# Two modulation vectors of a diffusion layer: matmul sets that take one weight tile each

## The chip, the cores and the metric

The kernel runs on one core of a Trainium2 chip. The time is device microseconds (us) of one launch. A core has TensorE (PE in the profile, its weight loads apart as PEld), VectorE (DVE), ScalarE (ACT), GpSimd (POOL) and a queue from which SyncE (SP) issues the transfers (DMA). TensorE writes its results into accumulator tiles of 128 partitions by 512 numbers.

## What is computed

One layer of a diffusion backbone over 256 latent tokens and 256 context tokens, of width 2048. A vector c of 2048 numbers is turned into six modulation vectors, and one for the context into two:

```python
mod = (jax.nn.silu(c) @ w_ada[i] + b_ada[i])[:, None, :]
mod_c = jax.nn.silu(c_ctx) @ w_ada[i] + b_ada[i]
sh1, sc1, g1, sh2, sc2, g2 = jnp.split(mod, N_MOD, axis=-1)
hc = rmsnorm(h_ctx, norm1_w[i]) * (1.0 + csc1) + csh1
s_f, s_b = ssd_branch(hc, zero_state, zero_state, None, lp, False)
hl = rmsnorm(x, norm1_w[i]) * (1.0 + sc1) + sh1
out_l, _, _ = token_mixer(hl, s_f, s_b, grid, lp)
x = x + g1 * out_l
hl2 = rmsnorm(x, norm2_w[i]) * (1.0 + sc2) + sh2
x = x + g2 * sqrelu_mlp(hl2, w_mlp1[i], w_mlp2[i])
return rmsnorm(x, final_norm_w)
```

The mixer has a long convolution and a state scan side by side. The MLP has 8192 hidden units. All is fp32 in size; a w_ada vector is a product of one row of 2048 with a matrix of 2048 by 2048 numbers (16 MB).

## The kernel before

Everything lies with channels on the 128 partitions and tokens along the tile. The large products (w_in, w_out, the MLP) stream 512 KB tiles of weights through the ring `raw` (5 tiles). Each is split into two reduced-precision parts (`hl`), with which TensorE does three matmuls of 128x128 weights by 256 tokens for each 128x128 block, into tiles `pg`. In the profile these are the rows `pg<-b,hl`; the text calls them the stream.

The modulation vectors come in three ways. The first two (and the context's) are made at the start by `ada_first` from `raw` and `ra` tiles. Vectors 0 and 1 (g1 and sh2) are made by `ada_vector` (line 422), and 2 and 3 by `vector_on_v` (line 443) on VectorE, whose multiply-adds are on line 459.

`ada_vector(v)` goes over 16 blocks kt of 128 inputs. For each it takes two tiles of the ring `ra` (5 tiles of 128x1024, which `vector_on_v` also uses), loads the 2048 output channels of the block into them (line 441), and calls `four` (line 413). That issues four fp32 matmuls, whose weights are 32 columns of the activated c (`csF`, through `cs32`) and whose moving operand is 512 channels of w_ada. The four write the four quarters of 32 partitions of one accumulator `pa` (ring of one tile), quarter j getting the channels 512 j to 512 j + 511, so that each uses its own 32 columns of the array. Only the first of the 32 rows of a quarter is used. In the text such a group of four is a set. After kt = 15 `columns` copies `pa` to a tile `ev` on ScalarE (line 287), and four small matmuls with the constant `sel2` turn rows into columns, in another tile `pa`. `finish` (line 405) adds the bias and writes `modR`, in which the other parts of the kernel read a vector as 16 columns.

`ada(n)` takes n steps of the two vectors at fixed places of the program: in the loops over scan units, hy units and z units, between 200 and 520 us. Where the instructions land is decided by a scheduler with a model of the chip's times: each engine takes the ready instruction with the lowest priority number. The sets get their number lowered by `FB` = 3000 (line 418), so they go in front of the stream as soon as the model holds their tiles landed. A load for `ra` is issued after the latest weight load of the stream that the program has reached (`tc.issue_after(main[0])`), from the one queue of SP.

Of the kernel before, what the change touches and what calls it, by code (L numbers as in the profile page):

```python
# [18 lines left out]
KT = 16  # L19
# [12 lines left out]
CS = {}  # L32
# [73 lines left out]
BOOST, HB, DB, FB, FH, ZB = 200, 100, 200, 3000, 400, 400  # L106
# [20 lines left out]
def build(tc, A, out):  # L127
    nc = tc.nc
    V, S, G, T = nc.vector, nc.scalar, nc.gpsimd, nc.tensor
# [13 lines left out]
    def mk(p, name, cols, bufs, dt=F32):  # L143
        def f(d=dt):
            return p.tile([128, cols], d, name=name, tag=name, bufs=bufs)
        return f
# [3 lines left out]
    ra = mk(wp, "ra", 1024, RA)  # L150
# [15 lines left out]
    def mm(o, l, r, start, stop):  # L166
        T.matmul(o, l, r, start=start, stop=stop)  # L167
# [30 lines left out]
    cst = cn.tile([128, NCS], F32, name="cst")  # L198
# [10 lines left out]
    def P(name, i, n=1):  # L209
        o = PC[name][0] + i  # L210
        return pc[:, o:o + n]
# [15 lines left out]
    csF = cn.tile([128, 64], F32, name="csT")  # L227
# [68 lines left out]
    def columns(ps, pt, sel="sel2"):  # L296
        ev = evac(ps, pt)
        return columns2(ev, pt, sel), ev
# [104 lines left out]
    modR = cn.tile([128, 4, KT], F32, name="modR")  # L403

    def finish(v, po, j0, nj):
        d = modR[:, v].rearrange("p (j m) -> p j m", j=4)[:, j0:j0 + nj]
        V.tensor_add(d, po.rearrange("p (m j) -> p j m", j=4)[:, 0:nj],
                     P("bada", 32 + 16 * v, 16).rearrange("p (j m) -> p j m", j=4)[:, j0:j0 + nj])
        if v == 2:
            V.scalar_tensor_tensor(d, d, 1.0, P("n2w", 0, 16).rearrange("p (j m) -> p j m", j=4)[:, j0:j0 + nj],  # L410
                                   op0=ALU.add, op1=ALU.mult)

    def four(pa, blocks, start, stop):


        p = tc.cur_priority
        for j, kt, w in blocks:
            tc.cur_priority = p - FB
            mm(pa[32 * j:32 * j + 32, :], cs32(kt), w, start, stop)
        tc.cur_priority = p  # L420

    def ada_vector(v):

        pa = pada()
        for kt in range(KT):
            ws = [ra(), ra()]
            for h in range(2):
                ada_load(ws[h], A["ada2"][v, kt][:, 1024 * h:1024 * h + 1024])
            four(pa, [(j, kt, ws[j // 2][:, 512 * (j % 2):512 * (j % 2) + 512]) for j in (2, 3, 0, 1)],
                 kt == 0, kt == KT - 1)  # L430
            yield
        po, _ = columns(pa, pada)
        finish(v, po, 0, 4)
        yield


# [2 lines left out]
    def ada_load(w, src):  # L439
        with tc.issue_after(main[0]) if main[0] else contextlib.nullcontext():  # L440
            nc.sync.dma_start(w, src)
# [31 lines left out]
    def cs32(kt):  # L473
        return csF[:, 2 * kt:2 * kt + 32]

    def ada_all():
        for v in range(2):
            yield from ada_vector(v)
# [60 lines left out]
    for n, (k0, nk) in enumerate(STEPS):  # L539
# [6 lines left out]
        po, _ = columns(pa, pada, "sel4" if nk == 4 else "selh")  # L546
# [12 lines left out]
        for nm, tiles, mod in (("C", cq, modC), ("L", xq, modL)):  # L559
            x = tiles[q][:, x0:x0 + xw]  # L560
            hi, lo = [t[:, x0:x0 + xw] for t in hq[nm]]
            v = x.rearrange("p (k t) -> p k t", k=nk)
            V.tensor_mul(v, v, rin[nm].unsqueeze(1).broadcast_to([128, nk, 256]))
            for k in range(nk):
                kt = k0 + k
# [25 lines left out]
        for u0 in range(0, 10, 8 // nk):  # L591
            nu = min(8 // nk, 10 - u0)
            w = (raw if n in WR else ra)()
# [3 lines left out]
            for uu in range(nu):  # L597
                u = u0 + uu
                ps = pgemm()
                for ci, nm in enumerate("CL"):  # L600
                    hi, lo = hq[nm]
                    o = ps[:, 256 * ci:256 * ci + 256]
                    for k in range(nk):
                        ws = slice(128 * (nk * uu + k), 128 * (nk * uu + k) + 128)
# [15 lines left out]
            for _ in range(2 if nk == 4 else NX):  # L620
                pa = next(nxt, None) or pa
# [58 lines left out]
    v, e, s, u2 = [spt[0][:, 128 * i:128 * i + 128] for i in range(4)]  # L680
# [327 lines left out]
    for q in range(4):  # L1008
        h, hi, lo = [b4w(d).rearrange("p (k t) -> p k t", t=WB) for d in (F32, F32R, F32R)]
# [162 lines left out]
```

## Time and profile before

| | us |
|---|---|
| median of three runs | 1403.72 (1402.85 to 1405.87) |
| the profiled execution | 1405.33 |
| its span, first to last instruction | 1403.5 |
| TensorE busy | 1369.3 (98%) |
| VectorE busy | 938.7 (67%) |
| ScalarE busy | 625.6 (45%) |
| queue q1, share of the 16 transfer engines | 65.3% |

The span is the time from the first to the last instruction in the trace; 1.8 us of the execution lie around it. Busy time of TensorE is the union of its matmul records. These overlap (each lasts some 0.28 us, while one starts every 0.12), so what a group of matmuls costs is read from starts and ends of neighbours, not from the length of one record. A page's idle time "before" a group is put down to what ended last.

### The profile page before, as it was taken

To read this page: it belongs to the slowest core of one execution; us is meant where nothing else is said; L and a number is where in the kernel's file an instruction comes from. 1 tells how busy PE (TensorE), PEld (TensorE's weight loads), DVE (VectorE), ACT (ScalarE), POOL (GpSimd) and SP (SyncE) were. 2 spreads that over 40 slices of the span, in tenths; PEclk is the share of its full clock that TensorE was granted. 3 is DMA by queue.
4 is the path that set the end of the run, shared out by engine and by line. 5 is a ranking of instruction groups with operands and counts; after the bars stand their busy time and mean duration, and the time that the engine had idled before them with its cause. 6 is when DMAs were issued, how large, how long until landed. Compare 5 with 4: busy or idle time off the path is not lost.

```text
span 1403.5 us, 26281 instructions
## 1 busy us (share of the span) xinstructions
PE 1369.3 (98%) x10936; PEld 1263.4 (90%) x10936; DVE 938.7 (67%) x1400; ACT 625.6 (45%) x922; POOL 9.6 (1%) x19
## 2 busy tenths in 40 slices
PE   5999999999999999999999999999999999999996
PEld 3467899887878788999999999999999999999996
DVE  7746578876886699878776665565565655565654
ACT  6432123565655344355444444443344433444452
POOL 0000000000000000000000000000000000000000
PEclk9999999999999999999999999999999999999998
DMA  9787776878786655557777875556555555555552
GB/s 351 251 322 276 261 252 211 302 263 294 277 277 237 224 180 174 165 161 254 274 258 253 280 245 174 181 179 192 187 182 183 185 186 183 182 185 182 186 185 87
DMA packets 86110, 311.56 MB, mean 222 GB/s; under 512 B 9863, under 2 KB 10216, under 8 KB 85992
## 3 DMA queue, kind: packets, MB, share of 16 engines
q1 hardware_dynamic: 85992, 309.90, 65.3%
q8 instruction: 85, 1.39, 0.4%
q14 instruction: 33, 0.27, 0.1%
HBM read 307.76 MB, written 2.10 MB: 221 GB/s over the span
## 4 chain that ended last, share of the span: by engine, by line
PE 91%; DMA 5%; DVE 2%; ACT 1%; SPq 0%; issue 0%; DVEq 0%; ACTq 0%
PE pg L167 78%; PE ps L167 8%; PE pa L167 5%; DMA ra<-in_ada_dram 3%; DMA raw<-in_ada_dram 1%; DMA xc<-in_cT_dram 1%; DVE hl L176 0%; DMA raw<-in_wS_dram 0%; PE ps L853 0%; ACT b L319 0%; PE ps L793 0%; DVE xc L1082 0%; DVE t L870 0%; DVE b L863 0%; DVE t L871 0%
## 5 line engine op out<-in xcount | busy, mean ns | idle before, releaser
L167 PEld LDWEIGHTS pg<-b,hl 128*128 128x128 f32 x9568 | 1153.6, 189 | 53.1 <-issue 46.2
L167 PE MATMUL pg<-b,hl 128*128 128x256 f32 (+1 forms) x9568 | 1183.8, 284 | 1.9 <-ACT hl L175 1.0
L175 ACT CAST hl<-raw 128x1024 fp32r<-128x1024 f32 x366 | 384.2, 1050 | 579.7 <-PE pg L167 471.5
L176 DVE TENSOR_TENSOR hl<-raw,hl 128x1024 fp32r<-128x1024 f32 x366 | 447.8, 1224 | 260.2 <-ACT hl L175 249.3
L459 DVE SCALAR_TENSOR_TENSOR ra<-ra,csT 128x1024 f32<-128x1024 f32 x60 | 76.7, 1279 | 0.4 <-DMA ra<-in_ada_dram 0.4
L1039 DVE TENSOR_TENSOR xc<-pg,CB 128x256 f32<-128x256 f32 x64 | 27.0, 423 | 32.8 <-PE pg L167 32.8
L778 ACT ACTIVATE rt<-cst,da 128x128 fp32r<-128x128 f32 x128 | 40.0, 391 | 9.9 <-PE ps L167 7.3
L167 PE MATMUL pa<-ra,csT 128*32 128x512 f32 x268 | 37.0, 604 | 2.6 <-DMA ra<-in_ada_dram 2.4
L167 PE MATMUL pa<-raw,csT 128*32 128x512 f32 x244 | 34.8, 617 | 2.8 <-DMA raw<-in_ada_dram 2.8
L1065 DVE SCALAR_TENSOR_TENSOR xc<-pg,modR,xc 128x256 f32<-128x256 f32 x32 | 15.5, 484 | 27.2 <-PE pg L167 27.2
L167 PE MATMUL ps<-b,cst 128*128 128x512 f32 x64 | 30.4, 596 | 0.0
L182 DVE TENSOR_TENSOR b<-xc,b 128x1024 fp32r<-128x1024 f32 x20 | 24.5, 1223 | 3.0 <-ACT b L181 3.0
L1041 ACT ACTIVATE xc<-xc 128x256 f32<-128x256 f32 x64 | 26.4, 413 | 0.1
L167 PE MATMUL ps<-b,b 128*128 128x512 f32 (+1 forms) x36 | 19.4, 674 | 5.0 <-ACT b L310 3.0
L181 ACT CAST b<-xc 128x1024 fp32r<-128x1024 f32 x20 | 21.0, 1049 | 7.0 <-DVE xc L931 3.3
L1040 DVE TENSOR_SCALAR xc<-xc,pg 128x256 f32<-128x256 f32 x64 | 22.8, 356 | 1.7
L167 PE MATMUL ps<-t,b 128*128 128x128 f32 (+1 forms) x128 | 22.4, 305 | 0.0
L619 DVE TENSOR_TENSOR xc<-pg,xc 128x512 f32<-128x512 f32 x14 | 9.6, 685 | 18.3 <-PE pg L167 18.3
L167 PEld LDWEIGHTS ps<-t,b 128*128 128x128 f32 x128 | 16.5, 191 | 4.2 <-issue 2.5
L167 PEld LDWEIGHTS ps<-b,b 128*128 128x128 f32 (+1 forms) x36 | 7.4, 228 | 14.0 <-issue 5.5
L175 ACT CAST hl<-ra 128x1024 fp32r<-128x1024 f32 (+1 forms) x11 | 10.7, 972 | 20.6 <-PE pg L167 16.7
L167 PEld LDWEIGHTS ps<-b,cst 128*128 128x128 f32 x64 | 10.9, 189 | 9.3 <-issue 6.6
(226 smaller groups left out, 737.6 us busy)
## 6 DMA issues: line engine op xcount, KB each, us to landing
raw<-in_w_dram SPq DMA_DIRECT2D x256, 512.0 KB, 4.1
ra<-in_ada_dram SPq DMA_DIRECT2D x131, 512.0 KB, 5.8
raw<-in_wL_dram SPq DMA_DIRECT2D x68, 512.0 KB, 5.3
raw<-in_ada_dram SPq DMA_DIRECT2D x61, 512.0 KB, 5.9
raw<-in_wO_dram SPq DMA_DIRECT2D x32, 512.0 KB, 4.1
raw<-in_wS_dram SPq DMA_DIRECT2D x10, 512.0 KB, 5.0
ra<-in_wS_dram SPq DMA_DIRECT2D x9, 512.0 KB, 7.6
xc<-in_xT_dram SPq DMA_DIRECT2D x8, 512.0 KB, 5.8
```

The lines of the kernel that those rows point to most:

```text
L167: T.matmul(o, l, r, start=start, stop=stop)
L175: S.copy(h[:, :cols], src)
L176: low[0] = V.tensor_sub(l[:, :cols], src, h[:, :cols]).ins
L181: S.copy(hi, src)
L182: V.tensor_sub(lo, src, hi)
L459: V.scalar_tensor_tensor(acc, old, ck, acc, op0=ALU.mult, op1=ALU.add)
L619: V.tensor_add(unit_acc(u), ps, old)
L778: S.mul(R[:, 256 * c + 128 * h:256 * c + 128 * h + 128], C("tle" if d == 0 else "tge"), dap[n][:, c, 16 * d + 2 * i + h:16 * d + 2 * i + h ...
L1039: V.tensor_mul(hv, ps[:, 0:256], r2)
L1040: V.tensor_scalar(hv, hv, ps[:, 256:257], 0.0, op0=ALU.add, op1=ALU.max)
L1041: S.activation(hv, hv, AF.Square)
L1065: V.scalar_tensor_tensor(xl, ps, modR[:, 3, i:i + 1], xl, op0=ALU.mult, op1=ALU.add)
```

## The change

For each kt and each half h of the 2048 channels one `ra` tile is taken and loaded. As soon as it is there, four matmuls of 256 columns take a quarter of it each, and write half h of the accumulator's columns in the four quarters of its partitions. The tile in memory is the same as before, so quarter j now holds other channels: 1024 h + 256 j and on. The addition at the end reorders them; it is `finish` written out for these vectors. Since two halves of one accumulator are now opened by different matmuls, four matmuls with zero weights (`csF[:, 32:64]`) over 512 columns of constants open the whole accumulator first, and no later matmul starts a sum.

```diff
     def ada_vector(v):
 
         pa = pada()
+        z = CS["fc"][0]
+        for j in range(4):
+            mm(pa[32 * j:32 * j + 32, :], csF[:, 32:64], cst[:, z:z + 512], True, False)
         for kt in range(KT):
-            ws = [ra(), ra()]
             for h in range(2):
-                ada_load(ws[h], A["ada2"][v, kt][:, 1024 * h:1024 * h + 1024])
-            four(pa, [(j, kt, ws[j // 2][:, 512 * (j % 2):512 * (j % 2) + 512]) for j in (2, 3, 0, 1)],
-                 kt == 0, kt == KT - 1)
+                w = ra()
+                ada_load(w, A["ada2"][v, kt][:, 1024 * h:1024 * h + 1024])
+                p = tc.cur_priority
+                tc.cur_priority = p - FB
+                for j in range(4):
+                    mm(pa[32 * j:32 * j + 32, 256 * h:256 * h + 256], cs32(kt), w[:, 256 * j:256 * j + 256],
+                       False, kt == KT - 1 and h == 1)
+                tc.cur_priority = p
             yield
         po, _ = columns(pa, pada)
-        finish(v, po, 0, 4)
+        V.tensor_add(modR[:, v].rearrange("p (h j m) -> p h m j", h=2, j=4),
+                     po.rearrange("p (h m j) -> p h m j", h=2, m=2),
+                     P("bada", 32 + 16 * v, 16).rearrange("p (h j m) -> p h m j", h=2, j=4))
         yield
```

The zero matmuls keep the ordinary priority; only the sets have the lowered number. The scheduler gives the whole program a new order. On TensorE, at the start of the second vector (v = 1), before; `pa<-ra,csT` is a set, `pg<-b,hl` the stream:

```order
L167 MATMUL pg<-b_1399,hl 128x256 x2
L167 MATMUL pg<-b_1400,hl 128x256
L167 MATMUL pa<-ra,csT 32x512 x4
L167 MATMUL pg<-b_1399,hl 128x256
L167 MATMUL pg<-b_1822,hl 128x256
```

And the same place now; `pa<-cst,csT` are the zero matmuls, `ps<-t,b` belongs to the scan:

```order
L167 MATMUL pg<-b_1822,hl 128x256
L167 MATMUL pa<-cst,csT 32x512
L167 MATMUL pg<-b_392,hl 128x256
L167 MATMUL pa<-cst,csT 32x512
L167 MATMUL ps<-t_3514,b_2221 128x256
L167 MATMUL pg<-b_393,hl 128x256
L167 MATMUL pa<-cst,csT 32x512
L167 MATMUL pg<-b_392,hl 128x256
L167 MATMUL pa<-cst,csT 32x512
L167 MATMUL pa<-ra,csT 32x256 x12
L167 MATMUL pg<-b_392,hl 128x256
```

The four zero matmuls of this vector stand apart, with one or two others between them, and three sets of 256 columns stand together behind the fourth. Those of the first vector stand as one `x4`. In all there are 64 sets in place of 32; the other 61 stand alone.

On the queue of SP, in the stretch of scan and hy units, before; `raw<-in_wL_dram` is the stream's weights, `ra<-in_ada_dram` the four vectors':

```order
L441 DMA ra<-in_ada_dram 128x1024
L632 DMA raw<-in_wL_dram 128x1024
L441 DMA ra<-in_ada_dram 128x1024
L632 DMA raw<-in_wL_dram 128x1024 x2
L441 DMA ra<-in_ada_dram 128x1024 x3
L632 DMA raw<-in_wL_dram 128x1024 x2
```

And now:

```order
L641 DMA raw<-in_wL_dram 128x1024
L450 DMA ra<-in_ada_dram 128x1024 x2
L641 DMA raw<-in_wL_dram 128x1024
L450 DMA ra<-in_ada_dram 128x1024
L641 DMA raw<-in_wL_dram 128x1024
```

The loads of the two kinds, which came in twos and threes, now alternate more evenly; their number and size are the same.

## Rows read from the trace of the kernel before

**Rows 1.** Busy time, share of the span and instructions, from the page.

```profile
PE 1369.3 (98%) x10936; PEld 1263.4 (90%) x10936; DVE 938.7 (67%) x1400; ACT 625.6 (45%) x922; POOL 9.6 (1%) x19
```

**Rows 2.** Windows: busy us of each engine (instructions), clock, transfer share, GB/s.

```profile
core 0: us, PE busy (x) PEld busy (x) DVE busy (x) ACT busy (x) POOL busy (x), PEclk, DMA share, GB/s
216.00:512.00 296.00, 293.44 (x2287) 247.56 (x2285) 226.22 (x408) 163.49 (x330) 0.00 (x0) 1.00 0.75 258
```

**Rows 3.** Tile pa from 216 to 512 us: durations min/median/max; idle ahead.

```profile
L167 PEld LDWEIGHTS pa<-ra,csT x256: 106/108/110, 216.4 to 510.5; 128*32 128x32 f32 x128
L167 PE MATMUL pa<-ra,csT x256: 592/605/617, 216.4 to 510.9; 128*32 128x512 f32 x128
...
  DMA ra<-in_ada_dram: 7.0, 13
```

**Rows 4.** Timeline around one set: start, length, records; then its weight loads.

```profile
216.08 0.40 PE L167 MATMUL pg<-b,hl 128*128 128x256 f32 x2
216.41 1.07 PE L167 MATMUL pa<-ra,csT 128*32 128x512 f32 x8
217.41 1.09 PE L167 MATMUL pg<-b,hl 128*128 128x256 f32 x7
...
217.41 1.01 PEld L167 LDWEIGHTS pg<-b,hl 128*128 128x128 f32 x8 [0.84 <-issue]
```

**Rows 5.** Timeline, 600 to 656 us: a long piece of pure stream.

```profile
600.05 55.73 PE L167 MATMUL pg<-b,hl 128*128 128x256 f32 x469
```

**Rows 6.** Timeline around two sets side by side, of the vectors made first.

```profile
108.30 0.40 PE L167 MATMUL pg<-b,hl 128*128 128x256 f32 x2
108.63 1.92 PE L167 MATMUL pa<-raw,csT 128*32 128x512 f32 x16
110.48 1.22 PE L167 MATMUL pg<-b,hl 128*128 128x256 f32 x8
```

**Rows 7.** Timeline around two fp32 matmuls on 64 columns each, 128 columns moving.

```profile
280.73 0.44 PE L167 MATMUL ps<-rt,t 128*64 128x128 f32 x4
281.10 0.51 PE L167 MATMUL ps<-rt,tri 128*128 128x512 f32 x1
```

**Rows 8.** Timeline where matmuls on 64 rows alternate with single stream matmuls.

```profile
205.16 0.38 PE L167 MATMUL pg<-b,hl 128*128 128x256 f32 x1
205.47 0.41 PE L167 MATMUL ps<-cst,t 64*128 64x32 f32 x2
205.80 0.39 PE L167 MATMUL pg<-b,hl 128*128 128x256 f32 x1
206.12 0.41 PE L167 MATMUL ps<-cst,t 64*128 64x32 f32 x2
```

**Rows 9.** Waits from 216 to 512 us: us in total, times, longest.

```profile
PE pa L167 <- DMA ra<-in_ada_dram: 2.4, 4, 0.9
...
PEld pa L167 <- DMA ra<-in_ada_dram: 4.6, 9, 1.1
...
SPq L441 <- PE pa L167: 39.9, 24, 3.7
```

**Rows 10.** Tile modR: vectors 0 and 1 written (L407), vector 1 read.

```profile
L1010 POOL COPY b<-modR x4: 191/657/1319, 531.2 to 575.6; 128x8 f32<-128x8 f32 x4
...
L407 DVE TENSOR_TENSOR modR<-pa,pc x2: 166/168/170, 381.5 to 516.2; 128x16 f32<-128x16 f32 x2
```

**Rows 11.** Timeline, 216.50 to 216.80 us: the four records of a first pass.

```profile
216.41 0.64 PE L167 MATMUL pa<-ra,csT 128*32 128x512 f32 x4
```

**Rows 12.** The chain of waits, 216 to 512 us, shares by line.

```profile
by line: PE pg L167 50.4%; PE ps L167 16.3%; DMA ra<-in_ada_dram 14.6%; PE pa L167 10.5%; DVE hl L176 0.9%; PE ps L793 0.9%; PE ps L853 0.8%; issue 0.7%; DVE b L863 0.6%; DVE b L864 0.6%; SPq L441 0.5%; DVE t L870 0.4%; DVE t L873 0.4%; DVE
```

## The prediction, made before the changed kernel ran

> **What bounds the kernel now.** I read the page's busy shares first: TensorE is busy 1369.3 of 1403.5 us [rows 1], so what lengthens TensorE's own work lengthens the kernel, unless it fills idle time of TensorE. Then the stretch in which the two sets are made, by windows: from 216 to 512 us TensorE is busy 293.4 of 296 us at a granted clock of 1.00 (2.4 GHz, the upper of its two levels), while the transfer engines are busy 0.75 and VectorE 226.2 us [rows 2]. So the stretch is TensorE's. Then the tile pa: 256 records in the stretch are 128 matmuls of 512 columns (each shows as two, since an fp32 matmul runs as two passes), that is 32 sets of four, and the idle time ahead of them by cause [rows 3].
>
> What one set of four costs stands in a narrow piece of the timeline [rows 4]. The last stream matmul ahead of it ends at 216.08 + 0.40 = 216.48, the seventh behind it at 217.41 + 1.09 = 218.50. These 2.02 us hold seven stream matmuls. In a pure stream one takes 55.73/469 = 0.119 us [rows 5], so seven take 0.83, and the set costs 2.02 − 0.83 = **1.19 us**. Where two such sets stand side by side, from 108.70 to 111.70 with eight stream matmuls behind, the two cost 3.00 − 0.95 = 2.05 us [rows 6]: the second costs 0.86 us. So 0.86 us is a set's columns, and the other **0.33 us** is paid for every visit: when TensorE goes from the stream's whole-array weights to weights on 32 columns and back. The weight loads tell the same: 0.84 us without one, as the next stream weights aren't loaded ahead [rows 4]. The Trainium skill says of this, in TensorEngine Tiling (Array Packing), Key Properties, that a change of the tiling mode "drains the TensorE". The trace agrees with its 0.84 us at the return, and the page names no price.
>
> **The change part by part.**
>
> *Sets of 256 columns.* For every block kt of 128 inputs the 4 matmuls of 512 columns become 2 sets of 4 with 256. The columns in sum are the same. Two views price a set of 256. By the neighbours it is half of 0.86 and one visit: 0.43 + 0.33 = 0.76 us. By another split form, two heads on 64 columns each with 128 columns moving, the way from its start to the next matmul's start is 281.10 − 280.73 = 0.37 us [rows 7], against 217.41 − 216.41 = 1.00 us with 512 [rows 4]. On the line between, 256 columns take 0.58, that is 0.42 less than 512, and the set costs 1.19 − 0.42 = 0.77 us. I take **0.77**. It holds where stream matmuls lie between the sets. In the new order on TensorE 61 of the 64 stand so (most behind 5 to 30 rows of other work) and three stand together at the start of the second vector.
>
> *The zero matmuls.* Each vector starts with four matmuls of 512 columns with zero weights. For the first vector they stand together: 1.19 us. For the second they stand apart, one or two other matmuls between them. One alone streams the same 512 columns twice and pays the same visit; it saves only the three short steps between neighbours, so about 1.17 us. That one stream matmul in between hides nothing is seen where a form of 64 rows alternates with single stream matmuls: the period is 0.65 us, of which 0.12 is the stream's, though the two short matmuls there move only 32 columns [rows 8]. So three cost 3.5 us. The fourth has the three sets behind it: 1.17 + 3 × 0.43 = 2.5 us.
>
> *Sum on TensorE.* Before: 32 × 1.19 = 38.1 us. After: 61 × 0.77 = 47.0, and 1.2, 3.5 and 2.5, in all 54.2 us. That is **+16.1 us**. Nothing else on TensorE is added. It is no idle time that these fill: the stretch has 2.6 us idle in all [rows 2].
>
> *Waits for tiles.* Before, a set waits for both its tiles; now each set waits for one, and that tile is free again one set earlier. At stake is what TensorE waits for: 2.4 us in 4 times on its own row, 4.6 us in 9 times on the weight loads, which hold part of the usual visit too [rows 9]. All of it gone gives −4.6. There are twice as many sets that can wait, so +4.6 on the other side, the same again. I take −1.5 us, near half of what the middle of the two rows holds: each pair now has 0.35 us more TensorE work around the same transfers, and the first of a pair needs only the older tile, but the second still needs what the set needed before.
>
> *The transfers.* As many, as large, from the same queue; they now alternate with the layer's weights more evenly. In the stretch the queue's ada entries wait 39.9 us in 24 times for a matmul on pa to free a tile [rows 9]. That gets shorter, but who would profit is TensorE, whose waits are priced above. VectorE's other two sets draw on the same five tiles; it has 70 us to spare in the stretch [rows 2].
>
> *The rest.* The copy of pa and the four short matmuls with sel2 stay. The addition writes the same 16 columns with another arrangement: 0.17 us as before. The second vector is ready at 516.2 and first read at 531.2 us [rows 10], and its last set lies at the same place among the other work, so 15 us of room stay. With the change the scheduler puts the whole order anew; behind 520 us TensorE's work is the same, and I allow 3 us either way for it.
>
> **Forecast.** 16.1 − 1.5 = +14.6 us. On the profiled execution: span 1403.5 + 14.6 = 1418.1, and its own 1405.33 becomes 1419.9. That execution is 1.6 us above the median of the runs, 1403.72, on which I put the forecast: **1418.3 us**.
>
> **The rivals.**
>
> *Columns alone.* If a visit is not paid per set, because the second set's weights can go in while other work drains, the 64 sets cost what 32 did, and only the zero matmuls are added: 1.2 + 3.5 + 1.2 = 5.9 us, less 1.5: 1408.1 us. For it: within a set the four run together, 0.64 us for four of which one lasts 0.617 [rows 3, 11]. Against it: the 0.33 us between a set alone and a second one beside another [rows 4, 6]. The Trainium skill would have it so: TensorE: Matmul & The Clock Gate, Measured speedup vs the span model, gives a pack the length of one matmul and about 4 ns for each further tile, and no price for entering or leaving. By that, 32 more sets are some 32 × 12 ns = 0.4 us, an estimate. The trace has about 7 ns for each further tile, and the visit besides. 8 in 100.
>
> *The second tile is waited for.* The new order puts the second set of many pairs only 5 to 8 rows behind the first, some 1 us, as if its tile came that soon. On the chip it may come later each time. Then waits double: +4.6 in place of −1.5, or 1403.7 + 16.1 + 4.6 = 1424.4 us. For it: the longest wait is 1.1 us [rows 9], and transfers in the stretch are dense at 258 GB/s [rows 2], by which 512 KB take 2.0 us. Against it: the same transfer was waited for before, in 13 of 32 sets at most. 12 in 100.
>
> *The ring of tiles sets the pace, and the time gets shorter.* The chain of waits gives transfers into ra 14.6% of the stretch, 43 us [rows 12]. If these were true length, then a tile freed after one set in place of two would cut the 39.9 us of the queue's waiting for pa [rows 9] by up to half, 20.0 us, and 16.1 − 20.0 gives 1399.8 us. It decides from the point where more than 16.1 us comes back. Against it: TensorE works through these transfers, and a chain that follows a late tile back to its issue counts time in which TensorE had other matmuls; its idle time for ra is 7.0 us with weight loads counted [rows 3]. 5 in 100.
>
> **How the numbers follow.** The forecast has 75 in 100. Its own spread is from the bounds of the waits, −4.6 and +4.6, and 3 us of reordering: 1412 to 1424 or so. The range 1410.5 to 1425.5 takes in the second rival and leaves out the first and the third. A measurement of this kernel tells about 0.2%, 2.8 us, from no change. Faster by that: 4 in 100, from the third rival. Same: 5 in 100, from the third's edge and half of the first. Slower: 91.
>
> **What would show it.** Of the profile after: sets of four 256-column matmuls from whose start to the next matmul are 0.58 us, and 0.77 us by the count of stream matmuls around; a gap of about 0.6 us in the weight loads at each; single zero matmuls with about 1 us each near the start of the second vector; the idle time for ra at 1 to 6 us. The place at which the second vector is added should move from 516 to about 531 us, and everything behind should follow at that distance. The prediction is wrong if a set alone costs under 0.65 us, if the move at the end of the stretch isn't kept to the end of the kernel, or if idle time for ra falls or grows by over 5 us.

## The result

The changed kernel takes 1418.54 us (median of 4 runs, 1416.5 to 1421.08) against 1404.39 for the kernel before (4 runs): the ratio is 1.0097, 95% interval 1.0085 to 1.0108. It is 14.2 us slower. The forecast was 1418.3 us. In a second comparison (e6 below) it was 1417.07 against 1403.68, 13.4 us slower. Of all executions told of here one, of e5, took 4692.27 us against 1412.4 to 1417.91 of its other five; e5's median is of all six, its ratio of those five.

The page of the changed kernel, busy time by engine. TensorE is busy 13.4 us more than in [rows 1], VectorE 1.3 us more and ScalarE 1.2 us less.

```profile
PE 1382.7 (98%) x11208; PEld 1269.5 (90%) x11208; DVE 940.0 (66%) x1400; ACT 624.4 (44%) x922; POOL 10.0 (1%) x19
```

The tile pa from 190 to 530 us, which answers to [rows 3]: 512 records of 256 columns in place of 256 of 512. Each lasts 0.379 us where it was 0.605. The 16 records of the zero matmuls are new. Idle time for tiles is 6.0 us where it was 7.0.

```profile
L167 PEld LDWEIGHTS pa<-ra,csT x512: 105/108/110, 211.0 to 528.0; 128*32 128x32 f32 x171
L167 PE MATMUL pa<-ra,csT x512: 378/379/404, 211.0 to 528.3; 128*32 128x256 f32 x171
L167 PEld LDWEIGHTS pa<-cst,csT x16: 106/108/109, 196.7 to 398.1; 128*32 128x32 f32 x16
L167 PE MATMUL pa<-cst,csT x16: 592/605/617, 196.7 to 398.6; 128*32 128x512 f32 x16
...
  DMA ra<-in_ada_dram: 6.0, 8
```

One set in the timeline of the changed kernel (start, length, records, idle time ahead), and then the weight loads behind it, which answer to [rows 4]:

```profile
210.48 0.64 PE L167 MATMUL pg<-b,hl 128*128 128x256 f32 x4
211.04 0.64 PE L167 MATMUL pa<-ra,csT 128*32 128x256 f32 x8
211.61 1.57 PE L167 MATMUL pg<-b,hl 128*128 128x256 f32 x11
```

```profile
211.61 0.77 PEld L167 LDWEIGHTS pg<-b,hl 128*128 128x128 f32 x6 [0.41 <-issue]
```

From the set's start to the next matmul 211.61 − 211.04 = 0.57 us go by, where the set of 512 columns took 1.00. Read as in the prediction: the stream ends at 211.12 ahead of the set and its eleventh matmul behind at 213.18. These 2.06 us hold eleven stream matmuls of 0.119, that is 1.31, and the set costs 0.75 us. Over the sets that stand in the stream, with the starts of the neighbours, the median is 0.765 us (1.193 before). The return to the stream leaves a gap of 0.41 us in the weight loads, where it was 0.84 and about 0.6 was expected. The gap has halved with the columns, while the visit costs what it did, so the length of the gap is not the visit's price.

The second vector's zero matmuls, which stand apart:

```profile
393.82 1.04 PE L167 MATMUL pa<-cst,csT 128*32 128x512 f32 x2
394.80 0.39 PE L167 MATMUL pg<-b,hl 128*128 128x256 f32 x1
395.11 1.05 PE L167 MATMUL pa<-cst,csT 128*32 128x512 f32 x2
396.09 0.70 PE L167 MATMUL ps<-t,b 128*128 128x256 f32 x2
396.44 0.47 PE L167 MATMUL pg<-b,hl 128*128 128x256 f32 x1
396.83 1.05 PE L167 MATMUL pa<-cst,csT 128*32 128x512 f32 x2
```

From one to the next with a single stream matmul between go 395.11 − 393.82 = 1.29 us, of which the stream matmul's own is 0.12: a zero matmul alone costs 1.17 us. It uses a quarter of the array's columns and costs nearly as much as the four of a set together.

That the lost time is lost in this stretch, and kept, is seen from where the same later work lies. Before, and then after, the updates of the residual in the output projection and in the last block of the MLP, with the starts of the first and the last of the 32:

```profile
L982 DVE SCALAR_TENSOR_TENSOR xc<-pg,modR,xc x32: 473/476/484, 555.5 to 650.6; 128x256 f32<-128x256 f32 x32
L1065 DVE SCALAR_TENSOR_TENSOR xc<-pg,modR,xc x32: 478/484/485, 1123.5 to 1390.1; 128x256 f32<-128x256 f32 x32
```

```profile
L991 DVE SCALAR_TENSOR_TENSOR xc<-pg,modR,xc x32: 471/476/487, 563.7 to 663.3; 128x256 f32<-128x256 f32 x32
L1074 DVE SCALAR_TENSOR_TENSOR xc<-pg,modR,xc x32: 479/484/486, 1135.7 to 1401.5; 128x256 f32<-128x256 f32 x32
...
L440 DVE TENSOR_TENSOR modR<-pa,pc x2: 172/174/176, 389.1 to 543.7; 128x16 f32<-128x16 f32 x2
```

The last of the projection is 663.3 − 650.6 = 12.7 us late, and the last of the kernel 11.4. The span grew by 11.2 us between the two profiled executions. That of the changed kernel is the fastest of its four, and that of the kernel before is 0.9 us above its median; the medians are 14.2 apart.

### The profile page after: what moved, and what is told of

It reads as the page before. It is cut to its first block, busy times and chain, and to the rows that moved or that the text cites. A ratio compares the mean times of both kernels' runs of the same rounds, so it can differ in the third digit from the quotient of the medians.

```text
span 1414.7 us, 26819 instructions
## 1 busy us (share of the span) xinstructions
PE 1382.7 (98%) x11208; PEld 1269.5 (90%) x11208; DVE 940.0 (66%) x1400; ACT 624.4 (44%) x922; POOL 10.0 (1%) x19
## 4 chain that ended last, share of the span: by engine, by line
PE 94%; DMA 4%; DVE 1%; ACT 1%; SPq 0%; issue 0%; DVEq 0%; ACTq 0%
PE pg L167 80%; PE ps L167 8%; PE pa L167 5%; DMA ra<-in_ada_dram 2%; DMA raw<-in_ada_dram 1%; DMA xc<-in_cT_dram 1%; PE ps L862 0%; DMA raw<-in_wS_dram 0%; PE ps L802 0%; ACT hl L175 0%; DVE xc L1091 0%; SPq L203 0%; ACT b L319 0%; DVE xc L572 0%; ACT L252 0%
## 5 line engine op out<-in xcount | busy, mean ns | idle before, releaser
L167 PE MATMUL pa<-ra,csT 128*32 128x256 f32 (+1 forms) x524 | 44.2, 395 | 2.5 <-DMA ra<-in_ada_dram 2.4
L167 PEld LDWEIGHTS pa<-ra,csT 128*32 128x32 f32 x524 | 11.2, 108 | 14.2 <-issue 3.7
L176 DVE TENSOR_TENSOR hl<-ra,hl 128x1024 fp32r<-128x1024 f32 (+1 forms) x11 | 12.4, 1124 | 10.8 <-ACT hl L175 5.1
```

Of the source, the lines that this page charges most:

```text
L176: low[0] = V.tensor_sub(l[:, :cols], src, h[:, :cols]).ins
```

## The experiments

They were made in three groups (e1 to e4, e5 and e6, e7 to e10), each beside its own runs of the kernel before, from whose median the column "time less before" counts. To read them, the time of one piece of work is split in the same manner for each trace: from the 750th to the 3320th matmul that isn't one of pa, so the same work from 176 to 544 us in the kernel before. A set's cost is the time from the last other matmul's start ahead of it to the second other matmul's start behind, less what these two take without a set. What a set started late by more than 0.2 us is counted as a wait. The rest is everything else. The last column is the rest without the stretches of low clock that are told of below the table. Forecast stands for the sum of the sets by the prices of the prediction (1.19, 0.77, 1.17 us; 0.86 for a second set of 512 columns beside another, half for 256).

| kernel | time less before | sets forecast | sets | waits | rest | rest at the upper clock |
|---|---|---|---|---|---|---|
| before | 0 | 38.1 | 37.9 | 3.2 | 327.1 | 325.6 |
| changed | +14.2 | 54.2 | 53.9 | 3.8 | 324.2 | 324.2 |
| e6, changed again | +13.4 | 54.2 | 53.9 | 3.3 | 325.8 | 324.3 |
| e1, no zero matmuls | +8.6 | 48.6 | 48.2 | 3.9 | 325.3 | 325.3 |
| e2, both halves in one visit | +6.2 | 44.0 | 44.4 | 6.6 | 324.6 | 324.6 |
| e3, zero matmuls alone | +8.7 | 44.0 | 44.2 | 5.3 | 324.8 | 324.8 |
| e4, zero matmuls together | +13.1 | 51.0 | 50.2 | 2.3 | 328.6 | 327.1 |
| e8, before with rings 6 and 5 | +11.5 | 38.1 | 38.1 | 2.4 | 333.0 | 331.1 |
| e9, changed with rings 6 and 5 | +17.6 | 54.2 | 53.9 | 1.7 | 325.6 | 324.1 |
| e7, two blocks in one visit, rings 6 and 5 | +8.5 | 32.8 | 32.4 | 2.5 | 334.9 | 333.1 |
| e10, the same, ring raw 4 | +18.5 | 32.8 | 32.4 | 0.8 | 344.5 | 340.4 |

e5 isn't in it, since five of its 16 visits lie behind the stretch. The traces are single executions, the first column is of medians.

The changed kernel and e6 are the same program, and its rest differs by 1.6 us between two executions. The granted clock accounts for that. The windows of the kernel before, of the changed kernel in the same place, and of e6, with columns as in [rows 2] (the clock is the third figure from the end):

```profile
207.90:211.20 3.30, 3.30 (x18) 3.30 (x17) 0.78 (x3) 0.62 (x2) 0.00 (x0) 0.50 0.73 243
208.90:212.20 3.30, 3.30 (x32) 2.75 (x31) 1.87 (x5) 0.62 (x2) 0.00 (x0) 1.00 0.72 218
208.50:211.80 3.30, 3.30 (x18) 3.30 (x17) 0.71 (x3) 0.62 (x2) 0.00 (x0) 0.50 0.77 217
```

At 0.50 (1.2 GHz, the lower of the two levels) the stream's matmuls start every 0.214 us in place of 0.119, so 44% of TensorE's busy time there is lost. That is 1.5 us here, and as much in e4 and e9; in e8 and e7 it is 1.9 and 1.8 us inside the stretch, in e10 4.1. All these figures are estimates from the two paces. In the kernel before and e6 the clock fell soon behind the short matmuls of [rows 8]; in the changed kernel's profiled execution the same matmuls ran and it stayed at 1.00. With this taken out, the changed kernel's three traces (e9 is the third) have a rest of 324.1 to 324.3 us.

### e1: the zero matmuls left out

The first set of each vector opens the whole accumulator itself, and the second half adds to it.

```diff
-        z = CS["fc"][0]
-        for j in range(4):
-            mm(pa[32 * j:32 * j + 32, :], csF[:, 32:64], cst[:, z:z + 512], True, False)
...
-                       False, kt == KT - 1 and h == 1)
+                       kt == 0 and h == 0, kt == KT - 1 and h == 1)
```

> The changed kernel without the zero matmuls: the first set of each vector starts the sum of the whole accumulator itself. Visit theory (0.33 us for every visit of the 32-column sets, 0.86 us for the columns of 512): the zero matmuls cost 1.2 us where four stand together and 3 x 1.17 + 0.9 us where they stand apart, so 5.6 us go: about 1412.9 us, 8.5 above the kernel before, all of it the 30 further visits of the sets (61 at 0.77 and three at 1.6 against 32 at 1.19, 10.5) less a few us of other order. Rival, the zero matmuls are the loss and halving the sets is free (columns alone): within 2 us of the kernel before, 1404.4.

It took 1412.08 us, ratio 1.0063 (1.0049 to 1.0078) to the kernel before, 8.6 us more. The zero matmuls are about 5 us of the loss, as 53.9 − 48.2 = 5.7 us of sets say. The larger part is left, so halving the sets isn't free: columns alone would have put this kernel within 2 us of the one before. The vectors come out right without the zero matmuls, so this part of the change bought nothing.

### e2: the same small sets, two to a visit

```diff
+            ws = [ra(), ra()]
             for h in range(2):
-                w = ra()
-                ada_load(w, A["ada2"][v, kt][:, 1024 * h:1024 * h + 1024])
+                ada_load(ws[h], A["ada2"][v, kt][:, 1024 * h:1024 * h + 1024])
+            p = tc.cur_priority
+            for h in (1, 0):
                 for j in range(4):
...
+                    mm(pa[32 * j:32 * j + 32, 256 * h:256 * h + 256], cs32(kt), ws[h][:, 256 * j:256 * j + 256],
+                       False, kt == KT - 1 and h == 0)
```

> The changed kernel, with both halves of a block issued together once both tiles are taken: eight matmuls of 256 columns in one visit, the zero matmuls kept. As many matmuls, loads of weights and columns as in the changed kernel, but 32 visits in place of 62. Visit theory: a visit costs 0.33 + 0.86 = 1.19 us as before, so 10.2 us go from the 54.2: about 1408.3 us. Rival, the cost is one of each matmul or weight load: no gain, 1418.5. By the wait theory (the second tile is waited for) the waits return to those of before, 3 us: 1418 as well.

It took 1409.7 us, ratio 1.0047 (1.0035 to 1.0059). The number of matmuls, of weight loads and of columns is that of the changed kernel. One visit in the trace of e2 and the next matmul, and the weight loads behind it:

```profile
257.50 1.07 PE L167 MATMUL pa<-ra,csT 128*32 128x256 f32 x16
258.50 0.94 PE L167 MATMUL ps<-b 128*128 128x128 f32 x6
...
258.50 0.74 PEld L167 LDWEIGHTS ps<-b 128*128 128x128 f32 x6 [0.41 <-issue]
```

Sixteen records of 256 columns take from start to next start 1.00 us, exactly what eight of 512 took in [rows 4]. So twice the number of matmuls and of weight loads costs nothing that shows; the visit does. And the gap in the weight loads is 0.41 us, half of that in [rows 4] at the same price: it goes with the columns of the last matmul. The sets fell by 9.5 us (forecast 10.2). In time 7.2 us came back of it (13.4 of e6 less 6.2, each against its own runs of the kernel before), since waits grew from 3.3 to 6.6 us: here each visit waits for two tiles again, and the tiles are also freed two at a time.

### e3: the zero matmuls alone, in the kernel before

```diff
+        z = CS["fc"][0]
+        for j in range(4):
+            mm(pa[32 * j:32 * j + 32, :], csF[:, 32:64], cst[:, z:z + 512], True, False)
...
-                 kt == 0, kt == KT - 1)
+                 False, kt == KT - 1)
```

> The kernel before with the zero matmuls alone added, its sets of 512 columns from two tiles left as they are. Visit theory: +1.2 us for the four that stand together and +4.7 for four that stand apart: 1410.3 us, if they land as in the changed kernel. Rival, they fill gaps: 1404.4 us.

It took 1412.24 us, ratio 1.0065 (1.0051 to 1.0078): 8.7 us more, where 5.9 were expected. The sets grew by 6.3 us, near the forecast of 5.9, and the waits by 2.1, which was not foreseen; the rest at the upper clock fell by 0.8. These make 7.6 us. The 1.1 us that are left are not accounted for; 7.6 lies within the interval of the ratio (7.2 to 10.9 us). The zero matmuls fill no gap.

### e4: the second vector's zero matmuls together

They get the lowered priority of the sets; in the trace the four then stand side by side ahead of three sets.

```diff
+        p = tc.cur_priority
+        tc.cur_priority = p - FB
         for j in range(4):
             mm(pa[32 * j:32 * j + 32, :], csF[:, 32:64], cst[:, z:z + 512], True, False)
+        tc.cur_priority = p
```

> The changed kernel with the zero matmuls at the lowered priority of the sets, so that the four of the second vector stand together as well. Visit theory: 4.4 us for the four apart become 1.2: 3.2 us less, 1415.3 us. Rival, a zero matmul costs the same alone or among others: 1418.5 us.

It took 1416.62 us, ratio 1.0094 (1.0081 to 1.0107), 13.1 us above the kernel before. In the trace the sets fell by 3.7 us, even a little more than said, and the waits by 1.0 to 1.5. In time that isn't seen: at the upper clock the rest is 2.8 to 2.9 us longer than in the two executions of the changed kernel. The scheduler ordered the whole stretch anew, and where the other work lost it I did not find. As a test of time it is inconclusive; as one of the price it agrees.

### e5: fewer visits, with the ring of five

If a visit costs 0.33 us, the kernel before should gain from fewer. Two neighbouring blocks are kept until all four tiles are there, and take one visit.

```diff
+            if kt % 2 == 0:
+                held = []
...
-            four(pa, [(j, kt, ws[j // 2][:, 512 * (j % 2):512 * (j % 2) + 512]) for j in (2, 3, 0, 1)],
-                 kt == 0, kt == KT - 1)
+            held.append((kt, ws))
+            if kt % 2:
+                for k, ww in held[::-1]:
+                    four(pa, [(j, k, ww[j // 2][:, 512 * (j % 2):512 * (j % 2) + 512]) for j in (2, 3, 0, 1)],
+                         k == 1, k == KT - 2)
```

> The kernel before, with the sets of two neighbouring blocks kt issued together: eight matmuls of 512 columns from four tiles in one visit, 16 visits in place of 32. Visit theory: 16 x 0.33 = 5.3 us less on TensorE, 1399.1 us if the waits for tiles stay at 3 us. Four of the five tiles of the ring are then held until the fourth is there, so the waits should grow; if they take it all back, 1404 us or more. Rival, columns alone: nothing to gain, 1404.4 us plus the longer waits.

It took 1414.31 us, ratio 1.0075 (1.006 to 1.0089). The waits took it back, and more. The timeline of e5 at the second vector, and the window from 512 to 545 us:

```profile
511.81 2.84 PE L167 MATMUL ps<-cst,b 128*128 128x128 f32 x24
521.20 3.23 PE L167 MATMUL pa<-ra,csT 128*32 128x512 f32 x16 [6.55 <-DMA ra<-in_ada_dram]
524.36 0.71 PE L167 MATMUL ps<-cst,small 128*128 128x128 f32 x4
524.91 0.50 PE L167 MATMUL ps<-cst,t 128*128 128x1 f32 x4
531.48 3.21 PE L167 MATMUL pa<-ra,csT 128*32 128x512 f32 x16 [6.07 <-DMA ra<-in_ada_dram]
```

```profile
512.00:545.00 33.00, 18.40 (x135) 11.40 (x135) 19.60 (x41) 6.07 (x11) 0.00 (x0) 0.79 0.63 217
```

The second vector's sets, which lay from 384 us on in the kernel before, start at 521 us, when the other work of the stretch is used up. TensorE stands idle 6.55 and 6.07 us for tiles. The granted clock falls to a mean of 0.79 in these 33 us, and the visits of 16 records take 3.23 and 3.21 us where one takes 1.92 at the upper clock [rows 6].

### e6: the changed kernel again

> The changed kernel once more, beside the others on the same chip: 14 us above the kernel before, 1418.5 us, with sets of 256 columns at 0.77 us each and some 4 us of waits for tiles.

It took 1417.07 us, ratio 1.0092 (1.0079 to 1.0105), with sets of 53.9 us and waits of 3.3.

### e7 to e10: a sixth tile

The room for a sixth tile in ra was taken from t2 (seven to five tiles; e7, e8, e9) or from raw (five to four; e10). e8 is the kernel before, e9 the changed one, e7 and e10 are e5. The edit, of e8:

```diff
-NB4, NRAW, RA, RT, T2 = 20, 5, 5, 4, 7
+NB4, NRAW, RA, RT, T2 = 20, 5, 6, 4, 5
```

> As e5_two_blocks, with six tiles in the ring ra in place of five and five in the ring t2 in place of seven, to make the room. In e5 the sets of the second vector came late, from 521 us on, and TensorE waited 15 us for their tiles. If the ring of five was the cause, the sets are spread over the stretch again, waits fall to 3 to 6 us and the 16 visits saved show: against the kernel before with the same rings (e8_before_six) 5 us less. If four tiles for one visit are waited for anyway, as slow as e5, 1414 us.

> The kernel before with six tiles in ra and five in t2, sets as they were. Control for e7 and e9: by the waits for tiles (3 us) at most 3 us can come back, less what the smaller t2 costs; 1402 to 1406 us.

> The changed kernel with six tiles in ra and five in t2. Visit theory: the cost of the sets stays, +16 us on TensorE, so 14 us above e8_before_six. Rival, the ring of tiles: with a sixth tile the changed kernel comes within 5 us of e8_before_six.

> As e7_two_blocks_six, but the room for the sixth tile is taken from the ring raw of the layer's weights, four in place of five, and t2 stays at seven. 16 visits fewer: about 1399 us if four tiles are enough for the stream, which has its weights landed in good time; above 1404 us if they are not.

e7 took 1412.27 us, ratio 1.0059 (1.0047 to 1.0071); e8 1415.25, 1.0085 (1.0073 to 1.0098); e9 1421.41, 1.0124 (1.0109 to 1.014); e10 1422.28, 1.0132 (1.0106 to 1.0157).

With the sixth tile e5's late sets are gone: waits are 2.5 us, and the sets cost 5.7 us less than in e8, 16 visits saved at 0.36 us each. e7 is 3.0 us faster than e8. So the ring of five was what held e5 up, and the price of a visit shows in the other direction too. But the room cost more than the visits gave: e8 is 11.5 us slower than the kernel before, and e10's smaller raw ring cost more still. No kernel here beats the one before.

The waits of the changed kernel fell by about 2 us with the sixth tile (1.7 after 3.3 to 3.8), and its sets stayed at 53.9 us. So tiles that come late are not what it loses by. Between e8 and e9, however, lie only 6.2 us in the medians, where I expected 14, and 1.6 us between the spans of the two profiled executions. The waits of TensorE from 500 to 680 us tell where it went. First e8, then e9:

```profile
PE pg L167 <- ACT b L181: 4.6, 2, 3.7
PE pg L167 <- ACT hl L175: 1.8, 2, 1.0
PE pg L167 <- DVE b L182: 1.7, 2, 0.9
PE ps L167 <- DVE small L263: 1.3, 1, 1.3
```

```profile
PE pg L167 <- ACT b L181: 0.9, 1, 0.9
PE pg L167 <- DVE b L182: 0.8, 1, 0.8
```

With these rings ScalarE and VectorE are late in e8 when the results of scan and convolution are split (lines 181 and 182), and TensorE waits 9.4 us for them and the small steps around. In e9 TensorE has 16 us more of its own work ahead of that place, and waits 1.7. Around these idle times e8's clock falls too; in e9 it doesn't there:

```profile
536.20:543.00 6.80, 4.36 (x18) 4.07 (x19) 4.83 (x11) 1.04 (x1) 0.19 (x1) 0.50 0.29 107
614.70:621.50 6.80, 6.04 (x29) 5.99 (x29) 1.98 (x2) 1.05 (x1) 0.00 (x0) 0.50 0.03 7
```

By the two paces these cost about 4.6 us. The 3200th matmul that isn't one of pa starts 16.0 us earlier in e8 than in e9, the 4000th 2.5 us earlier. So e8 loses 13.5 us in between, of which 7.7 are waits and 4.6 the clock. I read this as added work of TensorE that fills idle time there; no run tests that by itself, and the medians, 6.2 us apart, rest for the most part on executions without a trace.

## Why the prediction was right, point by point

**The bound.** TensorE was the limit of the stretch, and its added work lengthened the kernel. The move of 12.7 us at the end of the projection and 11.4 at the end of the kernel is the prediction's mark for it.

**The price of a set of 256 columns** was given as 0.77 us and is 0.765. Both ways to it, half the columns plus a visit of 0.33 us and the line between two other forms [rows 4, 6, 7], came out. e2 showed that it is the visit, and not the number of matmuls or weight loads. The third sign in the prediction, the gap of 0.84 us in the weight loads, was misread. Behind 256 columns it is 0.41 us (0.6 was forecast), also in e2, whose visits cost what those of 512 columns did. It shows that the stream's next weights come late, and not what a visit costs.

**The zero matmuls** were given 1.2, 3.5 and part of 2.5 us. One alone measures 1.17 us, and leaving them out takes 5.7 us from the sets and about 5 from the time.

**The sum on TensorE** was put at +16.1 us and measured +16.0 (53.9 − 37.9).

**The waits** were put at −1.5 us. This step failed, though by little: they went from 3.2 to 3.8 in one execution and 3.3 in the other. A set waits for one tile, but there are twice as many, and the longest wait became 1.4 us (3 waits of 2.4 us in all on TensorE's own row, where [rows 9] had 4 and the same sum):

```profile
PE pa L167 <- DMA ra<-in_ada_dram: 2.4, 3, 1.4
```

**The rest** was put at nothing, 3 us either way. It is 2.9 us shorter in the changed kernel's trace and 1.3 in e6. With the clock taken out of all three it is 1.3 to 1.4 us shorter, which I can't name. So 1.5 of the 2.9 us is only that the clock fell in the one execution and not in the other. Behind the stretch more comes back: 1.3 us between the 3300th and the 3450th matmul that isn't one of pa, and 1.1 between the 7500th and the 9000th. The second I can't name either, the first in part: the kernel before waits there 0.84 us for VectorE and 1.02 for ScalarE:

```profile
553.83 2.87 PE L167 MATMUL pg<-b,hl 128*128 128x256 f32 x22 [0.84 <-DVE hl L176]
557.72 17.27 PE L167 MATMUL pg<-b,hl 128*128 128x256 f32 x144 [1.02 <-ACT hl L175]
```

On the changed kernel's page the stream has only 0.8 us of such idle time in all.

**The hit of 0.2 us is luck in part.** The median of 1418.54 lies nearer to the forecast of 1418.3 than the parts deserve: waits that did not fall and a rest that shrank offset each other. Between the two profiled executions the span grew by 11.2 us and not by 14.6. The parts are 16.0 of sets, 0.6 of waits, −2.9 of the rest and −2.8 behind the stretch, which agree with 11.2 within 0.3 us.

**Marks that were wrong.** Besides the gap of 0.6 us: the second vector was to be ready at about 531 us. Its last set is at 528 us as expected, but the addition comes at 543.7: the short matmuls with sel2 are ordered later. Its first reader moved as well, from 531.2 to 546.4 us. TensorE did not wait for it: from 530 to 680 us it waits 0.8 us in all, for a split of the stream's weights. The move at the end of the stretch was kept for the most part: 13.9 us at the 3320th matmul, 11.2 at the end.

**The rivals.** Columns alone is refuted by e1 and e2. The second tile's waits did not double. The ring of tiles set no pace: the chain of waits gave it 14.6% of the stretch [rows 12], but the time grew, TensorE's waits for tiles are 3.2 to 3.8 us, and a sixth tile took only about 2 us of them away. The time of e9 says nothing of this by itself, since its smaller ring t2 made the kernel before slower too (e8).

## What to carry to other kernels

Price a group of small matmuls by what its neighbours lose, from the last matmul ahead to the steady stream behind, and split that price into columns and visits: here 0.86 us of columns and 0.33 us for going to another shape of weights and back. Where TensorE is full, work that comes in many small visits pays the visit each time, and an earlier start of each is worth only what TensorE really waited for the data (3 us here), not what a chain of waits shows for the transfers. The same added work cost less than half as much (6.2 us) where other engines had made TensorE idle right behind it (e9 against e8), so a change's price belongs to the kernel it was measured in. And before a difference of 1 or 2 us between two traces is explained, their granted clocks should be laid side by side: here 1.5 us of it was the clock.

## What the runs showed of the hardware that I had not expected

The visit's price didn't depend on how much work it held: with 8 records of 256 or 512 columns, or 16 of either, it is 0.33 to 0.36 us, if 512 columns in a set are priced at the 0.86 us of [rows 6]. The gap in the weight loads behind it did depend on that: 0.84 us behind 512 columns, 0.41 behind 256. A zero matmul on a quarter of the columns, alone between two others, costs 1.17 us, almost the 1.19 of four that run together. In e5 the granted clock fell in two idle times of TensorE, of 6.55 and 6.07 us, to a mean of 0.79 over 33 us, and the visits behind them took 3.23 and 3.21 us instead of 1.92. In the execution of the kernel before it fell to 0.50 at 207.9 us with no such idle time ahead: from 203 to 207.8 us TensorE was busy all of the 4.80 us.
